# Mixer A's query and key rows interleaved by head, so that their stores run dimension first

## The chip, the cores and the metric

The kernel runs on one core of a Trainium2 chip. The metric is device time in microseconds (us) of one execution. A tensor engine (PE), a vector engine (DVE), a scalar engine (ACT) and GpSimd (POOL) compute; SyncE (SP) issues nearly all transfers, in a fixed order, on one queue that 16 DMA engines serve.

## The reference

One layer of a streaming encoder is computed for 1024 prompt frames and 32 sample frames with 512 cached frames before them (T = 1056 rows in all, model width 1024). What matters here is mixer A's projection:

```
q_a = rope(rmsnorm(q_a.reshape(B, L, 8, 64), g_qn), pos)     # 8 heads of 64 dimensions
k_a = rope(rmsnorm(k_a.reshape(B, L, 8, 64), g_kn), pos)
def rope(x, pos):                                            # the first 32 dimensions with the last 32
    x1, x2 = xf[..., :half], xf[..., half:]
    return concatenate([x1 * cos - x2 * sin, x2 * cos + x1 * sin])
```

Mixer A keeps the best 256 keys of each query by an indexer's score (top-k) and does softmax attention over them; mixer B is stick-breaking attention over the same frames. Both outputs are gated, joined, and pass a feed-forward block. The keys of mixer A are also an output.

## The kernel before, in words

Everything is float32 arithmetic built of two float32r halves: a value is split into a rounded high part and the rest, and a product takes three matmuls (high by high, high weight by low, low weight by high).

Every instruction is written down first by a planner (class `Plan`, `record`) and issued later by its list scheduler (`run`, `issue`), so line 420 (`fn(*args, **kw)`) stands for nearly all rows of the profile and rows are told apart by the names of their tiles. The planner gives each operation a rank, an estimated cost and an estimated end; of the operations that are ready it issues that of the lowest rank. A transfer's estimated end comes from its size, times 1.6 where the on-chip side has at most 64 partitions. The number of DMA engines that a transfer uses does not enter. The result is one fixed order for each engine, and each engine works through its own in that order.

The order of the program around the change: the indexer, mixer B's q, k, v (`project_b`), the index scores and a first part of the top-k, then mixer A in four steps p = 0 to 3 (`project_a`: queries of heads 0 to 3, their keys, queries of heads 4 to 7, their keys), each with a `project_v`. Beside them run the rest of the top-k (`top_k`, which ends in the tiles `mask`) and some of the gate projections (`gate`, tile `gz`, stored to DRAM as `dg`). Then the pools of this stage (`proja`, `pre`, `top`, `rope`) are closed, their on-chip memory is given to the attention pools and to the next gates' tile `y`, and `attend` loads what was stored: `k<-dk`, `q<-dq`, `v<-dv`.

In `project_a` a 128-partition block holds one half (i = 0 or 1, the first or last 32 dimensions) of four heads. The names: PSUM tiles `s` hold the two raw halves; `sq` their squares; `t` and, for keys, `z` the rotated halves; `az` the pair (high, low) of a value, a ring of AZ = 4 buffers; `heads` a 128 x 4 matrix of zeros and ones that sums the squares by head; `dss` and `df` DRAM scratch for the sums and for the factors of the norm; `F` the factors spread over 128 partitions. For a key block the function `scaled` runs one step later: it loads F, multiplies z by it, stores z to the output `k_a`, splits it into az and stores both parts to `dk` (function `keep`). For a query block the norm's factor is applied later, in the softmax, and `keep` stores the rotated halves to `dq` at once. Each of the four blocks makes 12 stores from az (3 column ranges, 2 halves, 2 parts), and a key block 6 more to `k_a`. A buffer of az is written again only when both of its stores have landed.

Of the kernel before, what the change touches and what calls it, by code (L numbers as in the profile page):

```python
# [19 lines left out]
D = 1024  # L20
# [4 lines left out]
T = SEQ + DEC  # L25
# [403 lines left out]
class Layer:  # L429
# [748 lines left out]
    def project_a(self, p):  # L1178

        nc, pr, a = self.nc, self.pr, self.a  # L1180
        is_k, h0 = p % 2, 4 * (p // 2)
# [2 lines left out]
        units = [[self.unit(a["w_qka"][2 * p + i, j], pr if p % 2 else None) for j in range(2)] for i in range(2)]  # L1184
        C, S = self.tabs
        g = [self.gqk[:, 2 * is_k + i:2 * is_k + i + 1] for i in range(2)]
        dst = (self.dk if is_k else self.dq)[h0:h0 + 4].rearrange("g s (i e) t -> i g e s t", i=2)
        if is_k:
            z = nc.tile(pr, [128, 2, T], F32, "z", bufs=1)
        else:  # L1190
# [4 lines left out]
        def parts(hl, y):  # L1195
            nc.scalar.copy(hl[:, 0], y)
            nc.gpsimd.tensor_sub(hl[:, 1], y, hl.bitcast(F32)[:, 0])

        def keep(i, cs, hl):
            for j in range(2):  # L1200
                nc.sync.dma_start(dst[i, :, :, j, cs], hl.bitcast(F32)[:, j])

        for cs in (slice(0, 512), slice(512, 768), slice(768, T)):
# [10 lines left out]
            with nc.rank(FAST):  # L1214
# [3 lines left out]
                y = []  # L1218
                for i in range(2):
                    t = [tmp("t")[:, :n] for _ in range(2)]  # L1220
# [29 lines left out]
        if is_k:  # L1250
            with nc.rank(FAST):
# [4 lines left out]
                f = small("f")  # L1256
                self.rsqrt(f, v, HD, small)
                nc.sync.dma_start(self.df[p].rearrange("h (j t) -> (h j) t", j=32), f)
        else:
# [3 lines left out]
            f = nc.tile(pr, [128, NT, 4], F32, "f2", bufs=1)  # L1263
# [2 lines left out]

        def scaled():
            F = nc.tile(pr, [128, T], F32, "F", tag="vt", bufs=2)
            for h in range(4):
                nc.sync.dma_start(F[32 * h:32 * h + 32], self.df[p, h:h + 1].to_broadcast([32, T]))  # L1270
            out = self.o["k_a"].rearrange("(g i e) t -> i g e t", i=2, e=32)
            for cs in self.parts:
                for i in range(2):
                    y = z[:, i, cs]
                    nc.vector.tensor_mul(y, y, F[:, cs])
                    nc.sync.dma_start(out[i, h0:h0 + 4, :, cs], y)
                    hl = pair(cs.stop - cs.start)
                    parts(hl, y)
                    keep(i, cs, hl)
# [846 lines left out]
def _host_arrays(inp):  # L2126
    f = {k: np.asarray(v) for k, v in inp.items()}

    def units(w):
        k, m = w.shape  # L2130
        return np.ascontiguousarray(
            w.reshape(k // 512, 4, 128, m // 128, 128).transpose(3, 0, 2, 1, 4).reshape(m // 128, k // 512, 128, 512))

    x = np.concatenate([f["x_prompt"][0], f["x_sample"][0]], axis=0)
    out = {"xT": np.ascontiguousarray(x.T.reshape(KB, 128, T).transpose(1, 0, 2))}
    out["x"] = np.ascontiguousarray(x)
    w = f["w_in"]
    qa, ka, va, qi, ki, wi, qb, kb, vb, ga, gb = np.split(
        w, np.cumsum([512, 512, 512, 512, 64, 8, 512, 512, 512, 1024])[:10], axis=1)
    out["w_ia"] = np.ascontiguousarray(np.concatenate([qi[:, :256], ki, wi], axis=1).reshape(KB, 128, NI_A))  # L2140
    out["w_ib"] = np.ascontiguousarray(
        qi[:, 256:].reshape(4, 2, 128, NI_B).transpose(0, 2, 1, 3).reshape(4, 128, 512))
    out["w_qb"], out["w_kb"], out["w_vb"], out["w_va"] = units(qb), units(kb), units(vb), units(va)
    out["w_g"] = units(np.concatenate([ga, gb], axis=1))
    qk = np.stack([qa, ka]).reshape(2, D, 2, 4, 2, 32).transpose(1, 2, 0, 4, 3, 5)
    out["w_qka"] = units(np.ascontiguousarray(qk).reshape(D, 1024))
    out["w_ba"], out["w_bb"], out["w_out"] = units(f["w_branch_a"]), units(f["w_branch_b"]), units(f["w_out"])
    up, down = units(f["w_up"]), units(f["w_down"])
    out["w_up"] = np.ascontiguousarray(
        up.reshape(4, 2, 4, 2, 128, 512).transpose(1, 3, 0, 2, 4, 5).reshape(4, 16, 128, 512))  # L2150
    out["w_down"] = np.ascontiguousarray(
        down.reshape(4, 2, 4, 2, 128, 512).transpose(1, 3, 2, 0, 4, 5).reshape(4, 16, 128, 512))
    out["g_mix"] = np.ascontiguousarray(f["g_mix"].reshape(KB, 128).T)
    out["g_ffn"] = np.ascontiguousarray(f["g_ffn"].reshape(KB, 128).T)
    out["g_qk"] = np.ascontiguousarray(np.tile(np.stack([f["g_qn"], f["g_kn"]]).reshape(4, 32), (1, 4)).T)
    out["cki"] = np.ascontiguousarray(f["cache_k_idx"][0].T)
    for s, kn, vn in (("a", "cache_k_a", "cache_v_a"), ("b", "cache_k_sb", "cache_v_sb")):
        out["ck" + s] = np.ascontiguousarray(f[kn][0].transpose(1, 2, 0))
        out["cv" + s] = np.ascontiguousarray(f[vn][0].reshape(4, 128, H, HD).transpose(2, 1, 0, 3))
    inv = np.power(10000.0, -(np.arange(32, dtype=np.float32) / np.float32(32)).astype(np.float64)).astype(np.float32)  # L2160
    ang = (np.arange(NT * 128).astype(np.float32) - np.where(np.arange(NT * 128) >= SEQ, np.float32(SEQ - PAST),
                                                              np.float32(0)))[:, None] * inv[None, :]
    co, si = np.cos(ang.astype(np.float64)).astype(np.float32), np.sin(ang.astype(np.float64)).astype(np.float32)
    out["rope_c"] = np.ascontiguousarray(
        np.concatenate([co, co], axis=1).reshape(NT, 128, HD).transpose(1, 0, 2))
    out["rope_s"] = np.ascontiguousarray(
        np.concatenate([-si, si], axis=1).reshape(NT, 128, HD).transpose(1, 0, 2))
    out["rope_ct"] = np.ascontiguousarray(np.tile(co.T[:, :T], (4, 1)))
    out["rope_st"] = np.ascontiguousarray(np.tile(si.T[:, :T], (4, 1)))
    out["heads"] = (np.arange(128)[:, None] // 32 == np.arange(4)).astype(np.float32)  # L2170
    out["ident"] = np.eye(128, dtype=np.float32)
    i = np.arange(128)
    out["tri4"] = np.where(np.arange(DEC)[None, :] >= (i % DEC)[:, None], np.float32(NEG), np.float32(0)).astype(np.float32)
    out["tri"] = np.where(i[None, :] >= i[:, None], np.float32(1), np.float32(0)).astype(np.float32)
    return out
# [35 lines left out]
```

## Time and profile before

| | |
|---|---|
| median of 3 runs | 1746.93 us (1744.55 to 1747.72) |
| the profiled execution, its own time | 1746.15 us |
| its span in the profile | 1744.4 us |
| PE busy | 1685.4 us, 97% of the span |
| DVE, ACT, POOL busy | 1196.8, 1077.9, 915.1 us |
| moved by DMA | 303.96 MB, mean 174 GB/s |
| mixer A's projections and stores | some 290 to 535 us of the span |

The profile's first part gives an engine's busy time; its second cuts the span into 40 slices of 43.6 us and gives the busy share of each in tenths. PEclk is the granted clock of the tensor engine. A wait is written as the engine and tile that waited, an arrow, and what ended the wait.

### The profile page before, as it was taken

The page shows a single profiled execution, that of the slowest core. Times are in us where ns is not written, and L with a number is a line of the kernel's source. Part 1 is how long each engine was busy: PE and PEld are TensorE (multiplying, and loading weights), DVE is VectorE, ACT ScalarE, POOL GpSimd, SP SyncE. Part 2 cuts the span into 40 slices and gives each one's busy share as a digit, 9 for nine tenths or more (in the row PEclk, how much of TensorE's full clock was granted, in tenths as well). Part 3 has the DMA queues.
Part 4 walks back from the last instruction along what each step waited for, and adds up shares of the span by engine and source line. Part 5 has one row for each costly group of instructions (what it writes and reads, how often), then busy time and mean ns, then how long its engine had stood idle before and what let it go on. Part 6 is the DMA issues. An engine that isn't in the chain of part 4 may idle for free.

```text
span 1744.4 us, 33088 instructions
## 1 busy us (share of the span) xinstructions
PE 1685.4 (97%) x11260; PEld 1562.6 (90%) x11260; DVE 1196.8 (69%) x2585; ACT 1077.9 (62%) x2311; POOL 915.1 (52%) x805
## 2 busy tenths in 40 slices
PE   9999999995877999999999999999999999999999
PEld 8989998894866998998888888989899999999999
DVE  6567787884854655699867866765664775666667
ACT  7555798872214568767676657564745675747473
POOL 3342344444533438554354445747577794646563
PEclk9999999998988999999999999999999999999999
DMA  7353453333337767866647538665677656656565
GB/s 253 111 151 102 134 152 120 109 121 132 112 109 197 194 169 206 237 184 181 184 145 237 158 127 279 209 227 179 203 237 218 174 180 188 175 171 178 172 187 170
DMA packets 187979, 303.96 MB, mean 174 GB/s; under 512 B 29833, under 2 KB 59385, under 8 KB 187810
## 3 DMA queue, kind: packets, MB, share of 16 engines
q1 hardware_dynamic: 187378, 301.71, 57.2%
q8 instruction: 89, 1.46, 0.4%
q14 instruction: 80, 0.66, 0.1%
q10 hardware_dynamic: 432, 0.14, 0.0%
HBM read 213.89 MB, written 87.77 MB: 173 GB/s over the span
## 4 chain that ended last, share of the span: by engine, by line
PE 86%; DMA 5%; DVE 4%; issue 1%; SPq 1%; ACT 1%; POOL 1%; ACTq 0%; DVEq 0%; POOLq 0%
PE pj L420 62%; PE s L420 12%; PE t L420 5%; PE o L420 4%; PE pd L420 2%; SPq L420 1%; DMA wst<-w_qka 1%; DMA dk<-az 1%; DVE z L420 1%; DMA out_k_a<-z 1%; DMA dq<-az 0%; DMA dv<-vs 0%; DVE junk L420 0%; DMA k<-dk 0%; POOL wl L420 0%
## 5 line engine op out<-in xcount | busy, mean ns | idle before, releaser
L420 PE MATMUL pj<-xh,wh 128*128 128x272 f32 (+2 forms) x1802 | 595.1, 332 | 23.4 <-DVE gz L420 11.7
L420 PE MATMUL pj<-xh,wl 128*128 128x272 f32 (+2 forms) x1802 | 595.0, 331 | 0.5 <-POOL wl L420 0.3
L420 PE MATMUL pj<-xl,wh 128*128 128x272 f32 (+2 forms) x1802 | 594.6, 331 | 0.8 <-DVE xl L420 0.8
L420 POOL TENSOR_TENSOR wl<-wst,wh 128x512 fp32r<-128x512 f32 (+1 forms) x226 | 311.6, 1383 | 290.8 <-ACT wh L420 241.8
L420 PEld LDWEIGHTS pj<-xh,wh 128*128 128x128 f32 x1802 | 340.2, 189 | 52.0 <-DVE gz L420 12.3
L420 PEld LDWEIGHTS pj<-xl,wh 128*128 128x128 f32 x1802 | 340.7, 189 | 26.6 <-DVE xl L420 1.6
L420 PEld LDWEIGHTS pj<-xh,wl 128*128 128x128 f32 x1802 | 340.1, 189 | 26.7 <-POOL wl L420 1.1
L420 ACT CAST wh<-wst 128x512 fp32r<-128x512 f32 (+1 forms) x253 | 155.0, 616 | 137.9 <-PE pj L420 85.8
L420 POOL TENSOR_TENSOR wl<-raw,wh 128x512 fp32r<-128x512 f32 x111 | 146.9, 1330 | 84.3 <-ACT wh L420 76.4
L420 ACT CAST wh<-raw 128x512 fp32r<-128x512 f32 x169 | 103.9, 622 | 90.8 <-PE pj L420 69.3
L420 DVE TENSOR_TENSOR tt<-t,tt 128x512 fp32r<-128x512 f32 (+2 forms) x168 | 101.3, 620 | 30.9 <-ACT tt L420 29.9
L420 ACT ACTIVATE junk<-score,cand 128x384 bf16<-128x384 f32 (+1 forms) x124 | 116.0, 935 | 3.6 <-DVE cand L420 1.1
L420 ACT CAST tt<-t 128x512 fp32r<-128x512 f32 (+2 forms) x168 | 87.0, 538 | 44.7 <-PE o L420 23.3
L420 DVE TENSOR_TENSOR_SCAN p<-p,seen 128x384 f32<-128x384 f32 (+3 forms) x64 | 99.3, 1577 | 7.0 <-ACT p L420 4.0
L420 PE MATMUL pj<-gh,wh 128*128 128x272 f32 x352 | 101.2, 289 | 0.0
L420 PEld LDWEIGHTS o<-tt,v 128*128 128x128 f32 x640 | 92.7, 189 | 9.4 <-DVE tt L420 1.4
L420 PE MATMUL pj<-gl,wh 128*128 128x272 f32 x352 | 101.0, 288 | 0.0
L420 PE MATMUL pj<-gh,wl 128*128 128x272 f32 x352 | 100.9, 289 | 0.0
L420 PE MATMUL o<-tt,v 128*128 128x256 f32 (+1 forms) x640 | 99.6, 279 | 0.2
L420 PE MATMUL s<-k,q 128*128 128x384 f32 (+5 forms) x384 | 93.2, 352 | 0.9 <-DMA k<-dk 0.9
L420 PE MATMUL t<-ident,p 128*128 128x128 f32 x596 | 90.5, 275 | 0.0
L420 POOL TENSOR_SCALAR p<-p,nb 128x896 f32<-128x896 f32 (+6 forms) x66 | 52.0, 793 | 69.4 <-DVE nb L420 53.4
(441 smaller groups left out, 4003.9 us busy)
## 6 DMA issues: line engine op xcount, KB each, us to landing
q<-dq SPq DMA_DIRECT2D x64, 256.0 KB
raw<-w_down SPq DMA_DIRECT2D x60, 256.0 KB
raw<-w_up SPq DMA_DIRECT2D x57, 256.0 KB
k<-dk SPq DMA_DIRECT2D x48, 256.0 KB
v<-dv SPq DMA_DIRECT2D x48, 256.0 KB
wst<-w_g SPq DMA_DIRECT2D x42, 256.0 KB
dw_up<-raw SPq DMA_DIRECT2D x39, 256.0 KB
dw_down<-raw SPq DMA_DIRECT2D x39, 256.0 KB
```

The costliest lines, as they stand in the source:

```text
L420: fn(*args, **kw)
```

## The change

Rows of a block change their order. Before, partition 32g + e held dimension e of head g (of four): the heads one behind another, 32 rows each. Now partition 4e + g holds it: the four heads interleaved. The weights' columns, the norm's gains, the rotation's tables and `heads` are laid out anew on the host to fit. What lies in `dq`, `dk` and the output `k_a` is the same as before; the access pattern of their stores, which walks the 128 partitions in order, now goes over 32 dimensions, then 4 heads, then the columns, where it went over 4 heads, then 32 dimensions. The load of F, four transfers of 32 partitions, becomes one of 128. The matmul on `heads` and all elementwise work are the same in number and shape.

```diff
@@ project_a
-        dst = (self.dk if is_k else self.dq)[h0:h0 + 4].rearrange("g s (i e) t -> i g e s t", i=2)
+        dst = (self.dk if is_k else self.dq)[h0:h0 + 4].rearrange("g s (i e) t -> i e g s t", i=2)
@@ project_a, scaled
             F = nc.tile(pr, [128, T], F32, "F", tag="vt", bufs=2)
-            for h in range(4):
-                nc.sync.dma_start(F[32 * h:32 * h + 32], self.df[p, h:h + 1].to_broadcast([32, T]))
-            out = self.o["k_a"].rearrange("(g i e) t -> i g e t", i=2, e=32)
+            nc.sync.dma_start(F, self.df[p].unsqueeze(0).to_broadcast([32, 4, T]))
+            out = self.o["k_a"].rearrange("(g i e) t -> i e g t", i=2, e=32)
...
-                    nc.sync.dma_start(out[i, h0:h0 + 4, :, cs], y)
+                    nc.sync.dma_start(out[i, :, h0:h0 + 4, cs], y)
@@ _host_arrays
-    qk = np.stack([qa, ka]).reshape(2, D, 2, 4, 2, 32).transpose(1, 2, 0, 4, 3, 5)
+    qk = np.stack([qa, ka]).reshape(2, D, 2, 4, 2, 32).transpose(1, 2, 0, 4, 5, 3)
...
-    out["g_qk"] = np.ascontiguousarray(np.tile(np.stack([f["g_qn"], f["g_kn"]]).reshape(4, 32), (1, 4)).T)
+    out["g_qk"] = np.ascontiguousarray(np.repeat(np.stack([f["g_qn"], f["g_kn"]]).reshape(4, 32), 4, axis=1).T)
...
-    out["rope_ct"] = np.ascontiguousarray(np.tile(co.T[:, :T], (4, 1)))
-    out["rope_st"] = np.ascontiguousarray(np.tile(si.T[:, :T], (4, 1)))
-    out["heads"] = (np.arange(128)[:, None] // 32 == np.arange(4)).astype(np.float32)
+    out["rope_ct"] = np.ascontiguousarray(np.repeat(co.T[:, :T], 4, axis=0))
+    out["rope_st"] = np.ascontiguousarray(np.repeat(si.T[:, :T], 4, axis=0))
+    out["heads"] = (np.arange(128)[:, None] % 4 == np.arange(4)).astype(np.float32)
```

Since F's transfer is another to the planner, the fixed orders move too, from the first F on until well into the first attention heads; behind that they are the same. Two places matter later. The first is the end of SP's order for this stage, before the change: the last stores of p = 3 (dk from az, out_k_a from z, dg from gz) and the first load of attention (k from dk).

```order
L420 DMA dk<-az 4x32x272
L420 DMA dg<-gz 128x512
L420 DMA out_k_a<-z 4x32x272
L420 DMA dk<-az 4x32x272 x2
L420 DMA dg<-gz 128x272
L420 DMA out_k_a<-z 4x32x272
L420 DMA dk<-az 4x32x272
L420 DMA out_k_a<-z 4x32x272
L420 DMA dk<-az 4x32x272
L420 DMA dg<-gz 128x272
L420 DMA dk<-az 4x32x272 x2
L420 DMA k<-dk 128x512
```

The same end of SP's order with the change (mask_1553 is the mask of the sample rows).

```order
L420 DMA dg<-gz 128x272
L420 DMA out_k_a<-z 32x4x272
L420 DMA dk<-az 32x4x272 x2
L420 DMA out_k_a<-z 32x4x272
L420 DMA dk<-az 32x4x272
L420 DMA out_k_a<-z 32x4x272
L420 DMA dk<-az 32x4x272 x2
L420 DMA mask_1553<-mask_1553 32x544
L420 DMA dk<-az 32x4x272
L420 DMA k<-dk 128x512
```

The stores stand in nearly the same sequence with their leading sizes exchanged; the gate stores have moved ahead, and a copy of the sample rows' mask stands before the last store.

The second place is ACT's order about the end of the scaled keys of p = 1 and the first squares of p = 3, before the change. `az<-sq 128x512` is the one on which the matmul of `heads` for p = 3 waits.

```order
L420 COPY ss<-t 32x4
L420 CAST az<-z 128x272
L420 ACTIVATE sq<-s 128x512
L420 CAST az<-z 128x512
L420 CAST wh<-wst 128x512
L420 ACTIVATE rwq<-rvq 128x36
L420 CAST az<-z 128x272 x2
L420 ACTIVATE sq<-s 128x512
L420 CAST vs<-t 128x4x64 x2
L420 CAST az<-z 128x272
L420 ACTIVATE sq<-s 128x256
L420 CAST az<-sq 128x512
```

The same stretch of ACT's order with the change.

```order
L420 ACTIVATE sq<-s 128x512
L420 CAST az<-t 128x288
L420 CAST wh<-wst 128x512
L420 ACTIVATE rwq<-rvq 128x36
L420 CAST az<-z 128x512
L420 CAST vs<-t 128x4x64 x2
L420 ACTIVATE sq<-s 128x512
L420 CAST az<-z 128x272
L420 ACTIVATE sq<-s 128x256
L420 CAST az<-z 128x272
L420 CAST vs<-t 32x64 x2
L420 CAST az<-sq 128x512
```

Between the first square and `az<-sq` ACT copies four other pairs of az, before as after; one of them is now of t (queries of p = 2) where all four were of z.

## The prediction

> **What bounds the kernel now.** I read the page first, then busy time by stage, then the waits of the tensor engine, and last what its releasers waited for.
>
> ```profile
> span 1744.4 us, 33088 instructions
> PE   9999999995877999999999999999999999999999
> ```
>
> PE is full in all slices but four, the tenth to the thirteenth (about 392 to 567 us). In the table by stage the columns are the length, the busy time of PE, PEld, DVE, ACT and POOL (with instructions), the granted clock, the DMA share and GB/s.
>
> ```profile
> 320.00:395.00 75.00, 73.59 (x464) 65.94 (x463) 62.92 (x190) 60.85 (x140) 35.82 (x35) 0.98 0.36 114
> 395.00:460.00 65.00, 39.69 (x229) 34.41 (x228) 39.11 (x72) 11.45 (x31) 27.88 (x26) 0.82 0.33 108
> 460.00:500.00 40.00, 40.00 (x260) 36.62 (x259) 38.32 (x59) 8.16 (x19) 22.08 (x17) 1.00 0.48 140
> 500.00:540.00 40.00, 17.36 (x89) 15.71 (x88) 4.67 (x8) 3.27 (x5) 5.70 (x7) 0.74 0.51 150
> 540.00:750.00 210.00, 209.06 (x1399) 191.72 (x1398) 130.60 (x312) 146.10 (x329) 113.30 (x111) 1.00 0.73 198
> 750.00:1744.00 994.00, 989.22 (x6830) 929.03 (x6829) 700.96 (x1359) 617.11 (x1274) 584.33 (x478) 1.00 0.62 190
> ```
>
> Two stages leave PE idle: 65.00 - 39.69 = 25.3 us and 40.00 - 17.36 = 22.6 us, 47.9 us of the 59 us that the whole span has (1744.4 less 1685.4 busy). Behind 540 us there is nothing to gain: 5.7 us idle in 1204. The long waits of PE, in total, times and longest:
>
> ```profile
> PE t L420 <- ACT az L420: 23.2, 3, 20.0
> PE pj L420 <- DVE gz L420: 11.7, 1, 11.7
> PE pj L420 <- DVE y L420: 10.9, 1, 10.9
> ```
>
> The first waits for ACT's copy into az, the others for DVE to empty a PSUM bank into gz and y. What held those two engines, from their timelines (in brackets the idle time before the row, and its releaser):
>
> ```profile
> 416.65 0.62 ACT L420 CAST az<-z 128x512 fp32r<-128x512 f32 x1 [11.53 <-DMA dq<-az]
> 422.73 0.42 ACT L420 CAST az<-z 128x272 fp32r<-128x272 f32 x1 [3.22 <-DMA dk<-az]
> 428.19 0.42 ACT L420 CAST az<-z 128x272 fp32r<-128x272 f32 x1 [5.05 <-DMA dq<-az]
> 437.72 0.62 ACT L420 CAST az<-sq 128x512 fp32r<-128x512 f32 x1 [1.39 <-DMA dk<-az]
> 518.37 0.44 DVE L420 TENSOR_TENSOR gz<-pj,rb 128x272 f32<-128x272 f32 x1 [15.66 <-DMA dg<-gz]
> 533.56 1.28 ACT L420 ACT_TABLE_LOAD   x1 [16.95 <-DMA dk<-az]
> 533.62 0.69 DVE L420 TENSOR_TENSOR y<-pj,rb 128x512 f32<-128x512 f32 x1 [14.13 <-DMA q<-dq]
> ```
>
> So the stall at 418 to 438 is the ring of four az buffers: ACT loses 11.53 + 3.22 + 5.05 + 1.39 = 21.2 us to stores from it. At 507 to 519 gz waits for its own store, which stands on SP's queue among the dk stores; at 523 to 534 the next stage's memory is given out when the last dk store has landed. The last row is put down to q<-dq, but y lies in memory that the stage gives back, and ACT resumes on dk<-az at the same moment; I take dk as the cause. All three are one cause, stores from az and z. Why these are slow is in the DMA view, the mean busy share of 16 engines in 40 slices of a window, here 418 to 440 us:
>
> ```profile
> DMA  2225922222222222692298422222222222222222
> GB/s 103 106 94 205 350 107 88 92 90 90 90 92 101 99 93 95 212 322 93 97 164 317 175 87 98 88 83 101 101 97 97 104 104 87 100 92 89 89 87 87
> ```
>
> For most of it the share stays at 2 tenths and some 90 GB/s: about a quarter of the engines move data and the rest have none. Mixer B's stores of the same bytes, of 64 dimensions by 2 parts, run otherwise (100 to 106 us, two 256 KB stores issued at 101.5):
>
> ```profile
> DMA  7899364987989999999998999999999997510089
> GB/s 310 282 225 169 84 141 197 394 253 282 338 366 366 394 394 422 422 451 422 406 362 342 396 376 370 366 366 396 396 396 410 423 396 301 191 41 0 0 283 384
> ```
>
> The store whose slowest dimension is 4 uses a quarter of the engines, that with 64 uses all. [...]
>
> **The change, part by part.** The sum is made against the profiled execution's own 1746.15 us, 0.8 us under the median of the runs.
>
> *Stores of dq, dk and k_a.* Same number, bytes and contiguous runs; what changes is the engines that share them. A 256 KB store takes 2.9 us at 90 GB/s. Bounds: 0.6 us by the 64 x 2 stores (about 400 GB/s), and 2.9 us still, if the pattern doesn't spread. I take some 300 GB/s, 0.9 us, since weights and gate stores travel beside them. Stores that fill the queue also hold SP, which shows as the issue time (min/median/max ns) of the two kinds:
>
> ```profile
> L420 SPq DMA_DIRECT2D dk<-zz x24: 575/598/1177, 101.5 to 250.8; - x24
> L420 SPq DMA_DIRECT2D dk<-az x24: 508/1698/3401, 396.6 to 524.3; - x24
> ```
>
> The median should fall from 1698 to about 600 ns, and weight loads behind the stores leave SP earlier.
>
> *395 to 500 us.* With the stores out of the way the longer of PE and DVE is next. PE's work contains cold stretches: after a wait its matmuls run at half the rate.
>
> ```profile
> 395.21 0.39 PE L420 MATMUL s<-xl,wh 128*128 128x512 f32 x1
> 395.43 0.39 PE L420 MATMUL s<-xh,wl 128*128 128x512 f32 x1
> 398.62 0.27 PE L420 MATMUL t<-heads,az 128*128 128x4 f32 x1 [2.80 <-ACT az L420]
> ...
> 399.64 0.63 PE L420 MATMUL s<-xh,wl 128*128 128x512 f32 x1
> 400.07 0.63 PE L420 MATMUL s<-xh,wh 128*128 128x512 f32 x1
> ...
> 506.77 0.39 PE L420 MATMUL pj<-xh,wl 128*128 128x512 f32 x1
> 518.87 0.59 PE L420 MATMUL pj<-xh,wh 128*128 128x272 f32 x1 [11.71 <-DVE gz L420]
> ...
> 523.14 0.29 PE L420 MATMUL pj<-xh,wl 128*128 128x272 f32 x1
> 534.36 0.59 PE L420 MATMUL pj<-xh,wh 128*128 128x272 f32 x1 [10.93 <-DVE y L420]
> ```
>
> Starts lie 0.43 us apart where they were 0.22; over eight matmuls 1.6 us are lost. I estimate 2.0 us after the long stall from the same ratio, so PE's work at full clock is 39.69 - 3.6 + 40.00 = 76.1 us. DVE's is 39.11 + 38.32 = 77.4 us, much of it the top-k that must end in this stage. Both are nearly full, so some waits will stay; I leave 6 us, two like the 2.80 us wait with its cold matmuls, less a little. 77.4 + 6 = 83.4 in place of 105.0: **-21.6 us**. Bounds: 0 left gives -27.6; 16 left, as if half the stall came back on DVE, gives -12.
>
> [...]
>
> *500 to 540 us.* PE's work is 17.36 less its cold parts. Twelve matmuls from 518.87 and nineteen from 534.36 are 0.1 us slow each, 3.1 us, which leaves 14.3. When can y be written? The path there:
>
> ```profile
> 484.73 4.38 DMA F<-df
> 489.45 3.49 DVE L420 TENSOR_TENSOR z<-z,F 128x512 f32<-128x512 f32 x2
> 493.21 4.50 DVE L420 TENSOR_TENSOR z<-z,F 128x272 f32<-128x272 f32 x4
> 503.49 10.93 DMA dk<-az
> 519.42 8.77 DMA out_k_a<-z
> ```
>
> F lands at 489.1 and its last product ends at 497.7. One block's stores are 128 x 1056 x 4 B six times (four dk, two k_a), 3.24 MB: 36 us at 90 GB/s, which is what 497 to 533.6 shows, and 11 us at 300. Starting at 491 with gate stores between them, they end near 506. PE has work until 507.0 (the row at 506.77) and a block of 24 matmuls more (3.0 us at full clock) before it needs y: the stores land before PE gets there. What is late next is SP's order: k, v and q for attention follow the last store, and the mask's copy now stands before that store. I leave 3 us of wait and 1 of cold clock: 14.3 + 4 = 18.3 in place of 40: **-21.7 us**. Bounds: none left -25.7; nine left -17.
>
> *F as one transfer.* The issue of one of its parts:
>
> ```profile
> L420 SPq DMA_DIRECT2D F<-df x8: 303/424/834, 381.7 to 484.7; - x8
> ```
>
> SP issues one in place of four, 3 x 0.4 us saved on a queue that has waits anyway, and four landings become one. It lies in the chain that feeds the z products, but DVE is full there: counted at nothing; without that cover, up to 2 us gained. That all 16 engines now also carry 32 x 4 rows costs nothing that a row shows.
>
> *Rows interleaved on chip.* Matmuls, activations and products keep their shapes: 0.
>
> *The moved order.* Before 395 us the idle time is 1.4 us in 75; behind 540 us 0.9 in 210 and then an unchanged order. Nothing to gain, and a loss bounded by some us, since DVE there has room (130.60 of 210). I take 0.
>
> Sum: -21.6 - 21.7 = -43.3, 1746.15 - 43.3 = **1703**.
>
> **The rivals.** (1) Only one stall goes: in the first stage DVE's top-k, 77.4 us of work in a fixed order with PE's, takes the stores' place. For it: DVE is busy 38.32 of 40 us from 460 to 500. Against: in the stall itself ACT, not DVE, is the releaser. Then 1746 - 21.7 = 1724. (2) The stores don't spread, because the 32 x 4 pattern is cut in another way than 64 x 2. For it: no row shows it. Against: the quarter share at 4. The moved order alone remains: 1746, give or take 4. (3) Slower: the mask's copy before the last dk store. It waits for the end of the top-k on DVE and POOL; the last store, the loads for attention and y stand behind it on SP.
>
> ```profile
> 519.58 0.64 POOL L420 TENSOR_SCALAR mask<-pre 32x544 bf16<-32x544 f32 x1 [2.12 <-DVE pre L420]
> ```
>
> Before, this mask was ready only at 520.2, after a DVE wait for gz. It decides when it comes more than 43 us behind the last product; then 1751 or more. Against: the DVE steps left behind the last product take a few us, and the wait before them was the stores' own.
>
> **How the numbers follow.** Both stalls go, 0.78, between 1692 (all of 27.6 + 25.7, and a little before 395) and 1717 (12 + 17); one goes, 0.15, about 1724; no spread, 0.04; slower, 0.03. The range 1692 to 1722 holds the first and some of the second. About 0.2%, 3.5 us, is what a measurement tells from no change: faster 0.93, same 0.04, slower 0.03.
>
> **What would show it.** Right: the DMA share in these windows at 5 to 9 tenths where it was 2; dk's median issue near 0.6 us; PE's waits for az, gz and y under 5 us each; PE's idle time about 15 us in all; PEclk at 9 throughout. DVE as the releaser of new PE waits between 400 and 480 us would speak for rival 1, a share still at 2 for rival 2, SP waiting on the mask for rival 3. I would be wrong most easily in the first stage, where the 6 us left are a judgement.

## The result, and the profile after

The changed kernel takes 1689.59 us (median of 4 runs, 1688.17 to 1690.80); the kernel before, on the same chip, 1746.09 us. The ratio is 0.9676, 95% interval 0.9659 to 0.9693: 56.5 us less, where 43 were forecast. The time lies 2.4 us below the range's lower end of 1692; the forecast was wrong by its size, not its sign.

The page of the changed kernel, its span and the busy tenths of PE and granted clock:

```profile
span 1687.8 us, 33079 instructions
PE   9999999999999999999999999999999999999999
PEclk9999999999999999999999999999999999999999
```

The hole in the tenth to thirteenth slice is gone. PE is busy 1675.5 us of 1687.8 (before 1685.4 of 1744.4): of the 56.6 us of span, 46.7 were idle time and 9.9 busy time, most of it matmuls at half speed (some 6.9 us, an estimate from the rows: 1.6, 2.0 and 3.1 us by the prediction and 1.5 before 395 us, less 1.3 that is left). The mean granted clock rose from 0.986 to 0.999. The table by stage, with the columns of before:

```profile
320.00:395.00 75.00, 74.81 (x479) 67.31 (x478) 67.37 (x194) 59.34 (x138) 42.86 (x38) 1.00 0.41 131
395.00:460.00 65.00, 63.09 (x412) 57.29 (x411) 63.43 (x108) 14.54 (x36) 38.36 (x31) 1.00 0.42 140
460.00:500.00 40.00, 37.71 (x239) 34.80 (x238) 22.33 (x29) 15.09 (x32) 18.96 (x17) 0.96 0.74 222
500.00:540.00 40.00, 40.00 (x285) 37.40 (x284) 23.20 (x40) 23.52 (x59) 14.85 (x14) 1.00 0.69 185
```

From 395 to 460 us PE now does 412 matmuls where it did 229, and DVE is busy 63.43 of 65 us where it was 39.11. What is left of PE's waits in the whole span, longest first:

```profile
PE pj L420 <- DVE y L420: 2.3, 1, 2.3
PE s L420 <- DVE t L420: 1.3, 1, 1.3
PE o L420 <- DVE ss L420: 1.2, 1, 1.2
```

The wait for az (23.2 us) is not among them, that for gz fell from 11.7 to 0.3, that for y from 10.9 to 2.3. The issue of dk's stores (min/median/max ns) and DMA to landing in us, and the DMA view of 395 to 440 us:

```profile
L420 SPq DMA_DIRECT2D dk<-az x24: 518/550/888, 386.9 to 476.2; - x24
DMA to landing us min/median/max: 2.1/3.7/7.4
```

```profile
DMA  5999738988613413000000000002519800869910
GB/s 208 418 366 376 243 107 180 372 320 286 256 35 91 124 39 114 0 0 0 20 2 0 0 0 0 0 0 16 217 60 379 278 0 6 249 162 381 339 42 24
```

The long plain at 2 tenths has become bursts of 7 to 9 tenths and 250 to 420 GB/s, with little or nothing to move between them.

### The profile page after: what moved, and what is told of

Same layout as the page of the kernel before. It is cut to its first block, busy times and chain, and to the rows that moved or that the text cites. A ratio compares the mean times of both kernels' runs of the same rounds, so it can differ in the third digit from the quotient of the medians.

```text
span 1687.8 us, 33079 instructions
## 1 busy us (share of the span) xinstructions
PE 1675.5 (99%) x11260; PEld 1557.3 (92%) x11260; DVE 1198.7 (71%) x2585; ACT 1076.4 (64%) x2309; POOL 917.0 (54%) x805
## 4 chain that ended last, share of the span: by engine, by line
PE 93%; DVE 3%; DMA 1%; issue 1%; ACT 1%; SPq 1%; POOL 0%; ACTq 0%; DVEq 0%; POOLq 0%
PE pj L420 66%; PE s L420 14%; PE t L420 5%; PE o L420 5%; PE pd L420 3%; DVE pre L420 1%; SPq L420 1%; DMA q<-dq 0%; DMA vc<-cvb 0%; DMA F<-df 0%; DMA wst<-w_g 0%; DVE t L420 0%; DVE pj L420 0%; DVE pen L420 0%; DVE y L420 0%
## 5 line engine op out<-in xcount | busy, mean ns | idle before, releaser
L420 POOL TENSOR_TENSOR wl<-wst,wh 128x512 fp32r<-128x512 f32 (+1 forms) x226 | 316.0, 1403 | 265.8 <-ACT wh L420 230.2
```

## The experiments

All were run in three timed rounds beside the kernel before, whose medians were 1744.7 to 1745.8 us. "Head first" means stores of 4 x 32 rows as before, "dimension first" 32 x 4 as changed.

**Three lead sizes that were none.** lead4, lead8 and lead16 differ only in the split of 32:

```diff
-        dst = (...)[h0:h0 + 4].rearrange("g s (i e) t -> i e g s t", i=2)
+        dst = (...)[h0:h0 + 4].rearrange("g s (i a b) t -> i a b g s t", i=2, a=4)    # 8, 16
```

> The changed kernel, its instruction order and its single load of F unchanged; only the stores of dq, dk and k_a are written as 4 x 8 x 4 (slowest dimension 4 on the DRAM side, the same rows). Theory A (the spread of the stores is all of the gain): back to the time of before, 1746 us give or take 6, DMA share at 2 tenths and 90 GB/s in the stalls, median issue of dk near 1.7 us. Theory B (the moved order and the single F bring the 13 us beyond the forecast): 1733 us. Theory C (interleaved rows on chip, not the pattern's slowest size, make the spread): stays at 1690 us.

> The same with the stores written as 8 x 4 x 4 (slowest dimension 8). Theory A: half the engines, a 256 KB store in some 1.4 us; most of the wait is hidden by PE's other work, 1694 to 1702 us. Theory C: 1690 us.

> The same with the stores written as 16 x 2 x 4 (slowest dimension 16). Theory A: all 16 engines as with 32, 1690 us within 3. If the number of engines follows the slowest size beyond 16, or the fourth dimension costs, slower than 1693 us.

Measured: 1691.02, 1689.54 and 1689.55 us. These say nothing on the lead: a and b adjoin in DRAM, and in the traces the stores of all three have the shape of the changed kernel's, 32 x 4. lead4's dk stores issue and land like those, too:

```profile
L420 SPq DMA_DIRECT2D dk<-az x24: 518/550/1263, 387.4 to 477.5; - x24
DMA to landing us min/median/max: 2.1/3.6/7.7
```

So they speak neither against theory A nor for theory C. They serve as three repeats of the changed kernel, within 1.5 us of one another. The separation is made by the next two.

**Stores and order apart.** order_before keeps the changed stores and gives every engine the order of before; order_after keeps the stores of before and gives the order of the changed kernel. In the traces these orders are the same, instruction by instruction, on all five engines. F's load is not: order_before loads it in four parts, order_after in one that is head first, which the kernel before never had.

```diff
# order_before, from the changed kernel
-            nc.sync.dma_start(F, self.df[p].unsqueeze(0).to_broadcast([32, 4, T]))
+            for h in range(4):
+                nc.sync.dma_start(F[32 * h:32 * h + 32], self.df[p].unsqueeze(0).to_broadcast([8, 4, T]))
# order_after, from the kernel before
-            for h in range(4):
-                nc.sync.dma_start(F[32 * h:32 * h + 32], self.df[p, h:h + 1].to_broadcast([32, T]))
+            nc.sync.dma_start(F, self.df[p].unsqueeze(1).to_broadcast([4, 32, T]))
```

> The changed kernel with F loaded in four transfers of 32 partitions, so that every engine's order is that of the kernel before; the stores are 32 x 4 as changed. Theory A: 1690 us within 4. Theory B: 1700 us or more, the part beyond the forecast gone.

> The kernel before with its rows and its stores of 4 x 32 rows, but F loaded in one transfer of 4 x 32 rows, so that every engine's order is that of the changed kernel. It is the corner that lead4 was meant to give (there adjoining dimensions were merged and the stores went out as 32 x 4 again). Theory A (the spread of the stores is all of the gain, the order none): 1746 us give or take 6, share of 2 tenths in the stalls, median issue of dk near 1.7 us. Theory B (the moved order brings the 13 us beyond the forecast): 1733 us.

| median, us | stores head first | stores dimension first |
|---|---|---|
| order of before | 1745.5 (the kernel before) | 1687.7 (order_before) |
| order of the change | 1758.6 (order_after) | 1689.6 (the change) |

With either order the dimension-first pattern is worth more than the whole result: 57.8 and 69.0 us. The moved order brings nothing. With F's load it costs 1.9 us with dimension-first stores, and 13 with head-first ones (in which F, head first too, has a part, below). So theory A holds for the cause and theory B falls; A's own figure for order_after, 1746 give or take 6, was missed by 13. The waits of PE in order_after:

```profile
PE pj L420 <- DVE y L420: 30.3, 1, 30.3
PE t L420 <- ACT az L420: 21.4, 3, 20.6
PE t L420 <- DVE az L420: 8.0, 3, 6.5
```

The waits of before are back, that for y longer, and one for az through DVE is new (slow_F below has it too, 5.2 us). order_before is also the fastest kernel here: ratio 0.9663 (0.9644 to 0.9682) to before, and its 4 runs (1685.81 to 1688.46) hardly touch those of the change. Its PE has no wait for y among its longest:

```profile
PE o L420 <- DVE ss L420: 1.2, 1, 1.2
PE t L420 <- DVE small L420: 1.1, 1, 1.1
PE s L420 <- issue: 1.0, 1, 1.0
```

**Which stores.** In the order of the changed kernel one step's stores at a time go head first, into exchanged places.

```diff
-        dst = (...)[h0:h0 + 4].rearrange("g s (i e) t -> i e g s t", i=2)
+        dst = (...)[h0:h0 + 4].rearrange("g s (i e) t -> i g e s t" if p in (0,) else "g s (i e) t -> i e g s t", i=2)
# slow_p12: (1, 2), slow_p3: (3,), both with out_k_a as well; slow_ka: out_k_a alone, (1, 3)
```

> The changed kernel in its own order; only the stores of dq in step p = 0 are written head first (4 x 32 rows), so those rows of dq land in exchanged places and heads 0 to 3 of mixer A come out otherwise. Theory A1 (the stores of p = 0 held back the weights' loads before 320 us, a term the forecast left at 0): 1695.5 us, 6 more than the changed kernel. Theory A2 (these stores were hidden, as the forecast had it): 1690 us, and the early part of the gain comes from elsewhere.

> The same with the stores of p = 1 (dk and k_a) and p = 2 (dq) written head first, in exchanged places. By the forecast's first term, -21.6 us with bounds of 12 and 27.6: 1711 us (1702 to 1717), the stall of PE at the matmul of heads back. If the stalls aren't independent (a stall here gives the stores of p = 3 and the top-k time), less: under 1702.

> The same with only the stores of p = 3 (dk and k_a) written head first, in exchanged places. By the forecast's second term, -21.7 us with bounds of 17 and 25.7: 1711 us (1707 to 1716), the waits for gz and y back. If the stages add up, the three parts give back 1689.6 + 6 + 22 + 22 = some 1740 or more.

Measured: 1696.12, 1717.52 and 1717.09 us, that is 6.5, 27.9 and 27.5 us over the changed kernel; the last two lie just above the ranges given, to 1717 and 1716. All three keep the rows interleaved on chip, so theory C falls: it is the pattern of the stores that costs. slow_p0 settles the early part, A1. ACT's waits from 280 to 330 us, of slow_p0 and then of the kernel before:

```profile
ACT wh L420 <- DMA wst<-w_qka: 6.1, 3, 3.2
```

```profile
ACT wh L420 <- DMA wst<-w_qka: 5.4, 3, 3.2
```

The changed kernel has no such wait there. One load shows the difference: SP issues it at 292.09 us in the kernel before and at 292.19 in the changed one, where it takes 2.6 us to land. The copy that needs it, before and after:

```profile
298.27 0.62 ACT L420 CAST wh<-wst 128x512 fp32r<-128x512 f32 x1 [1.81 <-DMA wst<-w_qka]
```

```profile
296.47 0.61 ACT L420 CAST wh<-wst 128x512 fp32r<-128x512 f32 x1
```

So the load was not issued later, it landed later. Stores of p = 0 were issued just before and behind it (290.79 and 293.34 us in the kernel before); how they held it up is not shown, since no view has the engines one by one. The two others bring back the stalls one by one, each alone, the matmul of heads in slow_p12 and y in slow_p3:

```profile
PE t L420 <- ACT az L420: 23.7, 2, 21.1
PE pj L420 <- DVE y L420: 2.4, 1, 2.4
```

```profile
PE pj L420 <- DVE y L420: 29.3, 1, 29.3
PE o L420 <- DVE ss L420: 1.2, 1, 1.2
```

In slow_p3 the y wait is 29.3 us with q's loads spread as they always were. Its row for y names q<-dq, as the kernel before did; the changed kernel, with the same order, settles which it was. The row of y in slow_p3, then in the changed kernel the loads of q and the row of y:

```profile
503.97 0.69 DVE L420 TENSOR_TENSOR y<-pj,rb 128x512 f32<-128x512 f32 x1 [36.29 <-DMA q<-dq]
```

```profile
477.87 1.32 SPq L420 DMA_DIRECT2D q<-dq  x2
478.66 0.69 DVE L420 TENSOR_TENSOR y<-pj,rb 128x512 f32<-128x512 f32 x1 [9.59 <-DMA dk<-az]
```

There y is written 0.8 us after the first q load was issued, and such a load takes 4.2 us to land (median). So y doesn't wait for q; the reading of before, the last stores and not q, was right.

**k_a alone, F alone.** slow_ka writes only k_a head first; slow_F loads only F so (`unsqueeze(1).to_broadcast([4, 32, T])` in the changed kernel).

> The changed kernel in its own order; only the stores to k_a are written head first (4 x 32 rows), so the output's rows land in exchanged places; dq and dk stay spread. Theory by bytes (time goes with the bytes on the few engines): a third of the part of p = 3 (27.5 us) and a fifth of that of p = 1 and 2 (27.9 us), some 15 us, 1704 us. Theory by the ring (only stores that free az buffers or hold back y count, and k_a's are read from z): under 1696 us.

> The same with only the load of F written as 4 x 32 rows, so that F's rows stand for other heads and k_a and the keys come out otherwise. The three parts gave back 6.5 + 27.9 + 27.5 = 61.9 us, all of them with F head first 69.0. If the rest of 7 us is F's own landing on a quarter of the engines: 1696 us. If the parts make each other worse and F is hidden: 1690 us.

Measured: 1704.50 and 1699.71 us, 14.9 and 10.1 over the changed kernel. k_a's stores free no az buffer, yet cost what the theory by bytes gave (some 15). The ring alone doesn't explain the stalls. F was not hidden either, and cost more than the 7 us that were left for it. DVE's waits between 350 and 500 us in slow_F, and in the changed kernel:

```profile
DVE z L420 <- DMA F<-df: 9.4, 2, 5.6
```

```profile
DVE z L420 <- DMA F<-df: 1.0, 1, 1.0
```

Both F's together bring 8.4 us more of this wait. The four parts sum to 72.0 us (6.5 + 27.9 + 27.5 + 10.1), all at once 69.0: nearly additive.

**Slowest sizes of 31 and 16.** ka31 cuts each k_a store at 31 dimensions, ka16 at 16; all values keep their places. Two theories stood against each other: that a slowest size of 31 leaves a store fewer engines than 16 does, and theory E, that it doesn't.

```diff
-                    nc.sync.dma_start(out[i, :, h0:h0 + 4, cs], y)
+                    nc.sync.dma_start(out[i, 0:31, h0:h0 + 4, cs], y[0:124])
+                    nc.sync.dma_start(out[i, 31:32, h0:h0 + 4, cs], y[124:128])
```

> The changed kernel with each store to k_a cut in two, 31 dimensions by 4 heads and 1 by 4; all values in their places. [...] Theory E (as many engines as the slowest size has entries, up to 16): as ka16, within 2 us.

> The same cut at 16 and 16 dimensions, as the control of ka31 (the same number of stores, nearly the same order). Both theories: 16 engines for each part and 12 more issues of some 0.5 us on SP, 1690 to 1693 us.

Measured: 1765.37 and 1695.89 us. ka31 is slower than the kernel before (ratio 1.0122, 1.0107 to 1.0137). The DMA view of ka31, 470 to 520 us:

```profile
DMA  8447033094374315048330000056000000358400
GB/s 305 80 159 205 12 123 107 9 349 174 20 228 172 125 26 210 0 133 265 149 122 0 5 15 15 30 210 225 36 25 26 25 25 26 121 205 300 172 25 26
```

Where only these stores run, the rate is 25 to 26 GB/s and the share under 1 tenth. That is about one engine of 16, by an estimate: a sixteenth of the 366 to 423 GB/s that mixer B's stores reach at 9 tenths is 23 to 26, and four such give the 90 to 100 of before. So the rate doesn't follow the count of entries, and theory E falls: 31 entries are slower than 4. ka16's k_a stores land in 2.3 us (median), as the changed kernel's of 32 x 4 do. What it is about 31 is not shown. ka16 is 6.3 us over the change, more than the 0 to 3 expected: its wait for y is 6.2 us where the change has 2.3. Twelve more issues on SP may be one reason, its slightly other order another; they weren't tried apart.

## Why the prediction was right or wrong

The same instruction in both traces shows where time was gained. ACT's squares `az<-sq 128x512` of p = 1, before and after:

```profile
336.19 0.61 ACT L420 CAST az<-sq 128x512 fp32r<-128x512 f32 x1
```

```profile
330.28 0.61 ACT L420 CAST az<-sq 128x512 fp32r<-128x512 f32 x1
```

and of the changed kernel the first product of F for p = 3 and the start after y:

```profile
461.33 1.28 DVE L420 TENSOR_TENSOR z<-z,F 128x512 f32<-128x512 f32 x2
479.40 0.60 PE L420 MATMUL pj<-xh,wh 128*128 128x272 f32 x1 [2.29 <-DVE y L420]
```

The gain is 5.9 us by 330 us, 28.1 at the products (489.45 to 461.33), 55.0 at y (534.36 to 479.40) and 56.6 at the end.

*What bounds it, and why.* Right: the stores that left the DMA share at 2 tenths and some 90 GB/s were the one cause of all the long waits. The release of y by the last stores was right too.

*The stage before 395 us: the first step that failed.* It was taken at 0 in "the moved order", from 1.4 us of idle time in 75, with "a little before 395" as all that the range had for it. It was worth 5.9 us (slow_p0: 6.5). The stores of p = 0 were in the change like the others, but the sum was cut at 395 us, where the big stalls begin, and never looked at 280 to 320. Five short waits of PE between 302 and 323 us, 0.3 to 1.03 us each, make up its 2.9 us of idle time there (1.5 before 320, 1.4 behind it). One stretch at half speed, some 1.5 us lost, follows the last of them; the remaining 1.5 us I put down to the restarts around the waits, by difference. The kernel before, the last wait, two of the slow matmuls, and the stretch by stage (granted clock 0.50):

```profile
322.73 0.56 PE L420 MATMUL t<-heads,az 128*128 128x4 f32 x5 [1.03 <-DVE az L420]
324.48 0.63 PE L420 MATMUL s<-xl,wh 128*128 128x512 f32 x1
324.91 0.63 PE L420 MATMUL s<-xh,wl 128*128 128x512 f32 x1
323.78:327.19 3.41, 3.41 (x10) 2.63 (x9) 3.13 (x15) 2.84 (x9) 1.72 (x3) 0.50 0.58 168
```

*395 to 500 us and 500 to 540 us: mechanism right, the rest left over too large.* I left 6 and 4 us, 10 in all. The changed trace has waits of 4.2 us (for t 1.3, gz 0.3, az 0.3, y 2.3) and one cold stretch of 13 matmuls, 1.3 us: 5.5. The first term also took DVE's 77.4 us as the longer one; PE's 76.1 set the pace, 1.3 us more. DVE is full from 395 to 460 us (98%), so the warning was in place, but PE hardly waits for it. With the 5.9 before and 1.6 behind y, 43.3 + 4.5 + 1.3 + 5.9 + 1.6 = 56.6 us. That this meets the whole so exactly is in part chance: the cold matmuls behind y, nineteen before and thirteen now, 0.6 us, stand in two of the terms.

*F as one transfer, counted at nothing.* Right, as far as the runs show: order_before, with four parts, is no slower than the change. But the one transfer could also have been written head first, and then 10 us would have been lost (slow_F). The forecast didn't see F as a transfer that its pattern could slow: DVE's wait for it is 9.4 us in slow_F and 1.0 in the change.

*The moved order, taken as 0.* Within 2 us: it costs 1.9.

*The rivals.* That only one stall goes fell: the waits for az and for y both went. That the stores don't spread fell too. The mask is on the chain of work that ended last for 0.45 us of POOL, at 469.57 us, far from the 43 us that rival 3 needed.

*What would show it.* The issue time, the waits, the idle time (12.3 us) and the clock came as said. The share did not: I expected 5 to 9 tenths throughout, and the mean over 395 to 460 rose only from 0.33 to 0.42; the bursts in the DMA view leave gaps between them.

## What to carry to other kernels

Look at the DMA share during a wait: here a plain at 2 tenths with a full queue (a median issue of 1698 ns, 550 with the change) came from the pattern of the stores, not from little to move. Try another slowest dimension for them, even if rows must be laid out anew for it, and read the shape in the trace, since a split of 32 into adjoining parts came out as 32. Here stores with 32 in front reached 9 tenths (472 to 476 us of the changed kernel), as those with 64 did; with 4 they stayed at 2, with 31 under 1. The new layout was free on chip (DVE busy 1198.7 us for 1196.8, ACT 1076.4 for 1077.9, POOL 917.0 for 915.1), and 31 cost more than the whole gain (75.8 us). And when a cause is common to several places, sum over every place where it acts, not only where the waits are long.

## What the runs showed of the hardware that was not expected

Stores of 31 x 4 rows ran at 25 to 26 GB/s (ka31), slower than those of 4 x 32 at some 90. PE restarted at half speed behind a wait of 2.29 us in the changed kernel (0.23 us between starts in place of 0.13 for 13 matmuls), so the 2.80 us of the prediction is not the shortest such wait. In the kernel before the granted clock was 0.50 from 323.78 to 327.19 us, 1 us behind the restart from a wait of 1.03 us (322.73 us); behind one of 1.31 us in the changed kernel (411.93 us) it stayed at 1.00. What decides between these is not shown. With all transfers head first, F's single load among them, the order of the changed kernel loses 13 us to the other (order_after); with dimension-first ones the order of before loses nothing to it (order_before).
